# Layer 0's denominators: block sums on VectorE, and one block of row sums on TensorE in place of four

## The chip, the cores and the metric

One core of a Trainium2 chip runs the whole kernel. The time is the device time of one execution in microseconds. Three timed executions of the kernel before gave 911.12, 911.29 and 912.04 us; their median is 911.29 us. Below, PE is TensorE, DVE is VectorE, ACT is ScalarE, POOL is GpSimd and SP is SyncE, as the profile writes them.

## The reference, cut to what matters

The model has two layers over 512 tokens: layer 0 is an mLSTM mixer, layer 1 a gated linear attention. The change lies in layer 0, in the part behind the projections, which the reference writes for each of four heads in chunks:

```
s   = einsum('bhld,bhsd->bhls', q, k) * w_intra            # scores times decay weights
num = einsum('bhls,bhsv->bhlv', s, v) + ...                # numerator
den = sum(s, axis=-1) + ...                                # denominator: one number per row l
h   = num / maximum(abs(den), exp(-m_row))
```

After it come a normalisation over the 512 channels of the head, a gate with silu(z), and the output projection.

## The kernel before

The kernel takes all 512 tokens as one causal block. Tiles are held transposed: a score tile has the source position s on the 128 partitions and the target position t along the row. For a head h the causal scores are four blocks sb = 0 to 3 of source positions, kept one behind the other in one tile `A[h]` of 128 x 1280: block sb covers the targets from 128 sb to 511, so the blocks are 512, 384, 256 and 128 wide and begin at 0, 512, 896 and 1152 (`OFF`, `WID`).

All float32 products on TensorE are made from two parts, a rounded one (`hi`) and the remainder (`lo`). `split` (line 137) makes them: ACT copies the source into `hi`, then DVE subtracts `hi` from the source into `lo`. Weights that arrive by DMA are split in the same way (`whi`, `wlo`), three jobs ahead of their use.

The steps of a head, in the order in which the program writes them:

- `decay(h)` (line 661): PE forms log weights in four PSUM tiles, ACT turns them into weights `W[h]` by exp, and makes a row `EM[h]`.
- `weigh(h)` (line 678): one DVE multiplication of 128 x 1280, `A[h] = A[h] * W[h]`, with both inputs in SBUF.
- `split_scores(h)` (line 655): ACT copies `A[h]` into `shi`, DVE subtracts into `slo`.
- `split_v(h)` (line 681): ACT makes four `vhi`, DVE four `vlo`, of 128 x 512 each.
- `m_num(h)` (line 701): PE sums the rows of the scores with a matrix of ones: for each of the four blocks one matrix product with `shi` and one with `slo`, all into one PSUM tile `den`. ACT takes the absolute value `ad`, DVE the maximum with `EM[h]`. Then `attend` makes the four numerators `num`, of 12 products each; ACT squares each numerator, and POOL adds the four squares.
- `m_scale`, `m_skip` (lines 725, 735): DVE multiplies each numerator from PSUM with the gate; POOL makes four products of 128 x 512 from SBUF.
- `m_rstd(h)`, `m_y`, `y_split` (lines 742 to 768): PE sums the squares over the channels (`ssq`), DVE and ACT make the scale `rs`, DVE applies it in eight operations, and ACT and DVE split the result into `yhi` and `ylo`, the operand of the output projection `op`.

The four heads are interleaved with PE work that needs nothing of them: blocks `z` of the gate's projection (24 products of 512 columns each) behind heads 0, 1 and 2, and the first output products behind heads 2 and 3. Each engine does its own instructions in exactly the order of the program (`manual_schedule` for PE, ACT, DVE and POOL). The list of jobs sets that order: the DVE queue runs, after the numerators of head h, through a weight's `wlo`, then `weigh(h+1)` and `split_scores(h+1)`, then `rs` of head h. SBUF tiles of 128 x 512 come from one pool of 59 (`t2`), PSUM tiles from one of 8.

Of the kernel before, what the change touches and what calls it, by code (L numbers as in the profile page):

```python
# [10 lines left out]
F32R = mybir.dt.float32r  # L11
# [5 lines left out]
P = 128  # L17
T = 512
# [8 lines left out]
OFF = [0, 512, 896, 1152]  # L27
WID = [512, 384, 256, 128]
# [68 lines left out]
def tile_mlstm_gla(ctx, tc, xT, pvec, cst, wg, wgv, w_min, w_qk, w_v, w_mout,  # L97
                   w_gqk, w_gr, w_gu, w_gv, w_gz, w_gout, pw, lvl_masks, out):
    nc = tc.nc
# [9 lines left out]
    def t2(name, dt=F32):  # L109
        return tp.tile([P, T], dt, tag="t2", bufs=NT2, name=name)  # L110
# [4 lines left out]
    def t5(name, dt=F32):  # L115
        return tp.tile([P, SW], dt, tag="t5", bufs=7, name=name)

    def psum(name):
        return pp.tile([P, T], F32, tag="ps", bufs=8, name=name)

    def mm(out, lhsT, rhs, start, stop, more=False):

        nc.tensor.matmul(out, lhsT=lhsT, rhs=rhs, start=start, stop=stop, skip_group_check=more)  # L123
# [6 lines left out]
    def use(name):  # L130
        if table[0] != name:
            nc.scalar.preload_act_table_set(name)
            table[0] = name
# [3 lines left out]
    def split(hi, lo, src):  # L137
        nc.scalar.copy(hi, src)  # L138
        nc.vector.tensor_sub(lo, src, hi.bitcast(F32))  # L139
# [141 lines left out]
    ones_r = csr[:, P:2 * P]  # L281
# [131 lines left out]
    A = [None] * NH  # L413
# [239 lines left out]
    S, VS, EM = {}, {}, {}  # L653
# [2 lines left out]
        S[h] = t5("shi", F32R), t5("slo", F32R)  # L656
        split(*S[h], A[h])

    W = {}

    def decay(h):

        use(LNEXP)
        W[h] = t5("w")
        for sb in range(4):
# [4 lines left out]
            mm(ps[:, 0:P], ident_r, mneg_r, False, True)  # L670
            nc.scalar.activation(W[h][:, OFF[sb]:OFF[sb] + n], ps[:, 0:n], AF.Exp,
                                 bias=ac[:, sb * R16 + j:sb * R16 + j + 1])
# [4 lines left out]

    def weigh(h):
        nc.vector.tensor_mul(A[h], A[h], W[h])

    def split_v(h):
        VS[h] = t2s("vhi", 4, F32R), t2s("vlo", 4, F32R)
        for i in range(4):
            hi, lo = VS[h][0][i], VS[h][1][i]
            vm = vmean[:, 4 * h + i:4 * h + i + 1]
            nc.scalar.activation(hi, V[h][i], AF.Identity, bias=vm)
            nc.vector.scalar_tensor_tensor(lo, V[h][i], vm, hi.bitcast(F32), op0=ALU.add, op1=ALU.subtract)

    def attend(ps, h, vt):
        vs = slice(vt * P, (vt + 1) * P)  # L690
        (shi, slo), (vhi, vlo) = S[h], VS[h]
        for sb in range(4):
            o = ps[:, sb * P:T]
            sl = slice(OFF[sb], OFF[sb] + WID[sb])
            mm(o, vhi[sb][:, vs], shi[:, sl], sb == 0, False)
            mm(o, vhi[sb][:, vs], slo[:, sl], False, False)
            mm(o, vlo[sb][:, vs], shi[:, sl], False, sb == 3)
# [2 lines left out]

    def m_num(h):
        den = psum("den")
        shi, slo = S[h]
        for sb in range(4):
            sl = slice(OFF[sb], OFF[sb] + WID[sb])
            mm(den[:, sb * P:T], ones_r, shi[:, sl], sb == 0, False)
            mm(den[:, sb * P:T], ones_r, slo[:, sl], False, sb == 3)
        ad = t2("ad")
        nc.scalar.activation(ad, den, AF.Abs)
        nc.vector.tensor_max(ad, ad, EM[h])  # L710
        if steps:
            steps.pop(0)()
        NUM[h] = [psum("num") for _ in range(4)]
        sqs = []
        for vt in range(4):
            attend(NUM[h][vt], h, vt)
            sqs.append(t2("sq"))
            nc.scalar.square(sqs[vt], NUM[h][vt])
            if vt:
                nc.gpsimd.tensor_add(sqs[0], sqs[0], sqs[vt])  # L720
        ACC[h] = sqs[0]
        E2[h] = t2("e2")
        nc.scalar.activation(E2[h], ad, AF.Square, scale=EPS ** 0.5)
# [54 lines left out]
    job(gates3)  # L778
    z_job()
    job(lambda: (decay(0), weigh(0), split_scores(0), split_v(0)))  # L780
    job(lambda: (load_uc(0), load_uc(1)), n=0)
    z_job()
    job(lambda: load_v(1), n=0)
    job(lambda: (decay(1), steps.extend([lambda: None, lambda: (weigh(1), split_scores(1))])))

    def head_steps(h):
        m_rstd(h)
        if h + 2 < NH:
            load_v(h + 2)
            decay(h + 2)  # L790
        m_y(h, (0, 1))
        if h + 1 == NH:
            m_y(h, (2, 3))
            y_split(h, range(4))
        else:
            steps.extend([lambda: (split_v(h + 1), m_y(h, (2, 3)), silu_z(), load_uc(4 * h + 4), load_uc(4 * h + 5)),
                          lambda: None,
                          lambda: y_split(h, range(4))])
            if h + 2 < NH:
                steps.append(lambda: (weigh(h + 2), split_scores(h + 2)))  # L800
# [83 lines left out]
    for h in range(NH):  # L884
        job(lambda h=h: (m_num(h), m_scale(h), m_skip(h)), n=0)
        if h < NH - 1:
            z_job()
            job(lambda h=h: head_steps(h), n=0)
            for i in range((2, 3, 0)[h]):
                z_job(n=i < 2)  # L890
            if h == 2:
                for n in range(2):
                    out_full(n)
# [169 lines left out]
    def weights(what, c):  # L1063
        return {"P1": w_gout[0, 0, c], "P2": w_gout[0, 1, c], "P4": w_gout[1, 1, c], "P5": wsum["U", c],
                "P6": wsum["W", c], "P3": wsum["Z", c], "P7": wsum["R", c]}[what]

# [15 lines left out]
    def wsum_start(n, c):  # L1082
        nc.gpsimd.dma_start(wsum[n, c], {"U": w_gout[1, 0, c], "W": w_gout[0, 0, c], "Z": w_gout[0, 1, c],
                                       "R": w_gout[0, 0, c]}[n])

    def wsum_add(n, c):
        nc.gpsimd.dma_start(wsum[n, c], {"U": w_gout[1, 1, c], "W": wsum["U", c], "Z": wsum["W", c],
                                         "R": w_gout[1, 0, c]}[n], accum_op=ALU.add,
                            max_dma_last_dim=4096)
# [204 lines left out]
    bank, sums, parts = {}, {}, {}  # L1294
# [220 lines left out]
```

## Time and profile before

The profiled execution took 911.72 us, of which the profile's span is 910.0 us. TensorE's granted clock was at its upper level (2.4 GHz) nearly throughout.

| engine | busy us | share of the span | instructions |
|---|---|---|---|
| PE | 896.8 | 99% | 4624 |
| DVE | 628.8 | 69% | 917 |
| ACT | 539.2 | 59% | 917 |
| POOL | 182.7 | 20% | 163 |

The part that the change touches runs from about 307 to 428 us of the span, from head 0's weights to the first output products with head 3. A line of the timeline has the start in us, the duration in us, the engine, the line of the kernel, the operation, the tile written and the tiles read, and their shapes; a bracket at the end says how long the engine sat idle before and what ended that. Matrix products overlap in the pipeline, so what one costs is read from the start of one to the start of the next.

### The profile page before, as it was taken

The page shows a single profiled execution, that of the slowest core. Times are in us where ns is not written, and L with a number is a line of the kernel's source. Part 1 is how long each engine was busy: PE and PEld are TensorE (multiplying, and loading weights), DVE is VectorE, ACT ScalarE, POOL GpSimd, SP SyncE. Part 2 cuts the span into 40 slices and gives each one's busy share as a digit, 9 for nine tenths or more (in the row PEclk, how much of TensorE's full clock was granted, in tenths as well). Part 3 has the DMA queues.
Part 4 walks back from the last instruction along what each step waited for, and adds up shares of the span by engine and source line. Part 5 has one row for each costly group of instructions (what it writes and reads, how often), then busy time and mean ns, then how long its engine had stood idle before and what let it go on. Part 6 is the DMA issues. An engine that isn't in the chain of part 4 may idle for free. (4 is left out here: it accounts for less than half of the span.)

```text
span 910.0 us, 12523 instructions
## 1 busy us (share of the span) xinstructions
PE 896.8 (99%) x4624; PEld 756.1 (83%) x4624; DVE 628.8 (69%) x917; ACT 539.2 (59%) x917; POOL 182.7 (20%) x163
## 2 busy tenths in 40 slices
PE   9999999999999999999999999999999999999995
PEld 7887878878877888899999997777888888888884
DVE  6899798787695668788668748552446547478854
ACT  6866795766765657864666626455435354365642
POOL 0013564073140045135002310420000000000121
PEclk9999999999999999999999999999999999999998
DMA  8344364453432433322775694994344826383776
GB/s 320 117 163 142 125 200 136 156 189 108 149 116 94 138 116 116 115 85 88 236 226 187 210 346 150 246 240 119 116 139 127 257 101 208 115 281 108 262 277 140
DMA packets 54339, 153.88 MB, mean 169 GB/s; under 512 B 6176, under 2 KB 10656, under 8 KB 53984
## 3 DMA queue, kind: packets, MB, share of 16 engines
q1 hardware_dynamic: 48288, 126.58, 42.2%
q0 software_dynamic: 5696, 26.22, 10.9%
q8 instruction: 38, 0.62, 0.3%
q14 instruction: 29, 0.24, 0.1%
q10 hardware_dynamic: 288, 0.22, 0.1%
HBM read 133.07 MB, written 37.75 MB: 188 GB/s over the span
## 5 line engine op out<-in xcount | busy, mean ns | idle before, releaser
L139 DVE TENSOR_TENSOR wlo<-raw,whi 128x1024 fp32r<-128x1024 f32 (+1 forms) x146 | 186.3, 1283 | 96.6 <-ACT whi L138 95.8
L138 ACT CAST whi<-raw 128x1024 fp32r<-128x1024 f32 (+1 forms) x146 | 150.4, 1039 | 80.5 <-PE gv L123 24.3
L395 POOL TENSOR_TENSOR vp<-V,wv 128x512 f32<-128x512 f32 x56 | 86.2, 1560 | 173.4 <-ACT V L490 72.0
L123 PE MATMUL op<-yhi,whi 128*128 128x256 f32 x256 | 73.5, 287 | 0.0
L123 PE MATMUL op<-yhi,wlo 128*128 128x256 f32 x256 | 72.5, 283 | 0.4 <-DVE wlo L139 0.4
L123 PE MATMUL op<-ylo,whi 128*128 128x256 f32 x256 | 72.9, 285 | 0.0
L398 DVE SCALAR_TENSOR_TENSOR vp<-V,wv 128x512 f32<-128x512 f32 x72 | 68.0, 987 | 0.0
L163 POOL DMA_DIRECT2D whi<-wpP x8 | 4.3, 536 | 244.6 <-DMA raw<-in_w_gout 216.7
L123 PE MATMUL gz<-g2h,whi 128*128 128x512 f32 x128 | 51.6, 403 | 0.3 <-PEq L1180 0.3
L123 PE MATMUL qk<-chi,whi 128*128 128x512 f32 x128 | 50.1, 392 | 0.0
L123 PEld LDWEIGHTS op<-ylo,whi 128*128 128x128 f32 x256 | 49.1, 192 | 1.1 <-DVE ylo L139 0.6
L123 PE MATMUL gz<-g2h,wlo 128*128 128x512 f32 x128 | 49.9, 390 | 0.0
L123 PE MATMUL gz<-g2l,whi 128*128 128x512 f32 x128 | 49.9, 390 | 0.0
L123 PE MATMUL qk<-chi,wlo 128*128 128x512 f32 x128 | 49.8, 389 | 0.0
L123 PE MATMUL qk<-clo,whi 128*128 128x512 f32 x128 | 49.8, 389 | 0.0
L123 PE MATMUL gv<-whi,g2h 128*128 128x512 f32 x128 | 49.8, 389 | 0.0
L123 PE MATMUL gv<-wlo,g2h 128*128 128x512 f32 x128 | 49.8, 389 | 0.0
L123 PE MATMUL gv<-whi,g2l 128*128 128x512 f32 x128 | 49.8, 389 | 0.0
L123 PEld LDWEIGHTS op<-yhi,wlo 128*128 128x128 f32 x256 | 49.1, 192 | 0.6 <-DVE wlo L139 0.6
L123 PEld LDWEIGHTS op<-yhi,whi 128*128 128x128 f32 x256 | 49.1, 192 | 0.5 <-issue 0.5
L123 PE MATMUL z<-hhi,whi 128*128 128x512 f32 x112 | 44.1, 394 | 0.0
L123 PE MATMUL z<-hlo,whi 128*128 128x512 f32 x112 | 43.7, 390 | 0.0
(287 smaller groups left out, 2505.5 us busy)
## 6 DMA issues: line engine op xcount, KB each, us to landing
raw<-in_w_min SPq DMA_DIRECT2D x30, 512.0 KB, 3.8
raw<-in_w_mout SPq DMA_DIRECT2D x29, 512.0 KB, 4.2
wv<-in_wgv SPq DMA_DIRECT2D x32, 256.0 KB, 3.7
raw<-in_w_qk SPq DMA_DIRECT2D x16, 512.0 KB, 4.0
raw<-in_w_gqk SPq DMA_DIRECT2D x16, 512.0 KB, 4.3
raw<-in_w_gz SPq DMA_DIRECT2D x16, 512.0 KB, 4.7
raw<-in_w_gv SPq DMA_DIRECT2D x16, 512.0 KB, 4.1
raw<-in_w_v SPq DMA_DIRECT2D x8, 512.0 KB, 3.5
```

Source lines behind the costliest of these rows:

```text
L123: nc.tensor.matmul(out, lhsT=lhsT, rhs=rhs, start=start, stop=stop, skip_group_check=more)
L138: nc.scalar.copy(hi, src)
L139: nc.vector.tensor_sub(lo, src, hi.bitcast(F32))
L163: nc.gpsimd.dma_start(to, of)
L395: nc.gpsimd.tensor_mul(j, V[h][i], w)
L398: nc.vector.scalar_tensor_tensor(j, V[h][i], 1.0, w, op0=ALU.mult, op1=ALU.mult, accum_out=o)
```

## The change

`weigh(h)` gets six operations more. DVE adds the four blocks of the weighted scores where their targets overlap: the targets from 128 on, of block 0 and block 1 (384 columns), then block 2 (256 columns), then block 3 (128 columns). The sum `d` is split into `dsh` (ACT) and `dsl` (DVE), 384 columns each. These stand ahead of `split_scores(h)` in the order of ACT and of DVE. In `m_num(h)`, PE sums the rows of `dsh` and `dsl` for the targets from 128 on, and those of `shi` and `slo` for the first 128 targets, which block 0 alone reaches: four products in place of eight. Three more tiles of the `t2` pool are in use per head.

```
     def weigh(h):
         nc.vector.tensor_mul(A[h], A[h], W[h])
+        d, hi, lo = t2("ds"), t2("dsh", F32R), t2("dsl", F32R)
+        nc.vector.tensor_add(d[:, P:], A[h][:, P:T], A[h][:, OFF[1]:OFF[2]])
+        nc.vector.tensor_add(d[:, 2 * P:], d[:, 2 * P:], A[h][:, OFF[2]:OFF[3]])
+        nc.vector.tensor_add(d[:, 3 * P:], d[:, 3 * P:], A[h][:, OFF[3]:])
+        split(hi[:, P:], lo[:, P:], d[:, P:])
+        DS[h] = hi, lo
...
     def m_num(h):
         den = psum("den")
-        shi, slo = S[h]
-        for sb in range(4):
-            sl = slice(OFF[sb], OFF[sb] + WID[sb])
-            mm(den[:, sb * P:T], ones_r, shi[:, sl], sb == 0, False)
-            mm(den[:, sb * P:T], ones_r, slo[:, sl], False, sb == 3)
+        for sl, parts in ((slice(P, T), DS[h]), (slice(0, P), S[h])):
+            for i in range(2):
+                mm(den[:, sl], ones_r, parts[i][:, sl], i == 0, i == 1)
```

## Rows read from the trace of the kernel before

**Rows 1.** The page: span, and busy time of each engine.
```profile
span 910.0 us, 12523 instructions
...
PE 896.8 (99%) x4624; PEld 756.1 (83%) x4624; DVE 628.8 (69%) x917; ACT 539.2 (59%) x917; POOL 182.7 (20%) x163
```
**Rows 2.** Timeline of PE, head 1: the denominator, and `vlo`'s last product.
```profile
342.66 0.39 PE L123 MATMUL den<-shi,csr 128*128 128x512 f32 x1
...
343.12 0.33 PE L123 MATMUL den<-shi,csr 128*128 128x384 f32 x1
...
343.46 0.28 PE L123 MATMUL den<-shi,csr 128*128 128x256 f32 x1
...
343.70 0.22 PE L123 MATMUL den<-shi,csr 128*128 128x128 f32 x1
...
345.68 0.27 PE L123 MATMUL num<-shi,vlo 128*128 128x128 f32 x1
```
**Rows 3.** Groups by line and shape: DVE and ACT operations by their width.
```profile
L139 DVE TENSOR_TENSOR ylo<-hc,yhi 128x512 fp32r<-128x512 f32 x16 | 10.0, 687 | 0.0
...
L310 DVE TENSOR_TENSOR sq<-sq 128x256 f32<-128x256 f32 x14 | 5.9, 422 | 0.8 <-ACT sq L307 0.7
...
L547 ACT ACTIVATE A<-sc 128x384 f32<-128x384 f32 x4 | 1.9, 484 | 1.5 <-PE sc L123 1.5
```
**Rows 4.** Timeline of head 0: DVE, then PE's first use of the last `vlo`.
```profile
312.34 1.49 DVE L139 TENSOR_TENSOR slo<-A,shi 128x1280 fp32r<-128x1280 f32 x1 [1.33 <-ACT shi L138]
313.75 2.74 DVE L687 SCALAR_TENSOR_TENSOR vlo<-Vr,vmean,vhi 128x512 fp32r<-128x512 f32 x4
...
318.18 0.27 PE L123 MATMUL num<-shi,vlo 128*128 128x128 f32 x1
```
**Rows 5.** Timeline of DVE, head 1.
```profile
328.53 2.58 DVE L679 TENSOR_TENSOR A<-A,w 128x1280 f32<-128x1280 f32 x1
332.49 2.37 DVE L139 TENSOR_TENSOR slo<-A,shi 128x1280 fp32r<-128x1280 f32 x1 [1.38 <-ACT shi L138]
...
343.20 0.74 DVE L687 SCALAR_TENSOR_TENSOR vlo<-Vr,vmean,vhi 128x512 fp32r<-128x512 f32 x1
```
**Rows 6.** Timeline of POOL, head 1: the last three products of `m_skip(0)`.
```profile
327.48 2.28 POOL L740 TENSOR_TENSOR z<-ucr,z 128x512 f32<-128x512 f32 x1
...
329.73 2.53 POOL L740 TENSOR_TENSOR z<-ucr,z 128x512 f32<-128x512 f32 x1
...
332.22 1.28 POOL L740 TENSOR_TENSOR z<-ucr,z 128x512 f32<-128x512 f32 x1
```
**Rows 7.** Timeline of DVE and POOL around head 3: short DVE operations beside POOL.
```profile
407.78 2.50 DVE L139 TENSOR_TENSOR ylo<-hc,yhi 128x512 fp32r<-128x512 f32 x4
...
408.88 2.55 POOL L720 TENSOR_TENSOR sq<-sq 128x512 f32<-128x512 f32 x1 [14.84 <-ACT sq L718]
...
418.20 1.79 DVE L758 TENSOR_TENSOR hc<-hc,rs 128x512 f32<-128x512 f32 x1
```
**Rows 8.** Timeline of head 1: squares on ACT, their sum on POOL, `ssq` on PE.
```profile
350.87 2.07 ACT L718 ACTIVATE sq<-num 128x512 f32<-128x512 f32 x4
...
354.79 2.17 POOL L720 TENSOR_TENSOR sq<-sq 128x512 f32<-128x512 f32 x1
...
357.05 1.08 PE L123 MATMUL ssq<-sq,cs 128*128 128x512 f32 x2
```
**Rows 9.** Timeline of head 2: `vlo` on DVE, and PE's first use of the last.
```profile
368.34 2.73 DVE L687 SCALAR_TENSOR_TENSOR vlo<-Vr,vmean,vhi 128x512 fp32r<-128x512 f32 x4
...
378.68 0.27 PE L123 MATMUL num<-shi,vlo 128*128 128x128 f32 x1
```
**Rows 10.** Timeline behind head 3: POOL's last sum, `ssq`, PE's wait in the output.
```profile
412.88 1.29 POOL L720 TENSOR_TENSOR sq<-sq 128x512 f32<-128x512 f32 x1
...
414.24 1.11 PE L123 MATMUL ssq<-sq,cs 128*128 128x512 f32 x2
...
428.30 0.38 PE L123 MATMUL op<-yhi,wlo 128*128 128x256 f32 x1 [0.39 <-DVE wlo L139]
```

More of the change, by code (lines that the diff above doesn't have):

```diff
@@ L657, in split_scores @@
         split(*S[h], A[h])
-    W = {}
+    W, DS = {}, {}
     def decay(h):
```

## The prediction, made before the changed kernel ran

> **What bounds the kernel now.** I read the page first: TensorE is busy for 896.8 us of a span of 910.0 us [rows 1]. The reader is to see there that no other engine is near its limit, and that time taken from TensorE's queue comes off the end, as long as TensorE doesn't begin to wait. So the question is not what the added DVE and ACT work costs, but whether TensorE waits for it somewhere. For that I went from the groups by line to the timelines of the four heads, and noted for each thing that TensorE takes from the other engines how long before its use it is ready: its cover. In head 0 the last `vlo` is ready at 313.75 + 2.74 = 316.49 and first used at 318.18 [rows 4], a cover of 1.69 us. In head 1 it is ready at 343.94 and used at 345.68 [rows 2, 5]: 1.74 us. In head 2: 371.07 and 378.68 [rows 9], 7.6 us. The sum of squares that `ssq` takes is far tighter: POOL ends it at 356.96 and TensorE begins `ssq` at 357.05 [rows 8], 0.09 us later; behind head 3 the two are 414.17 and 414.24 [rows 10], 0.07 us. TensorE shows no wait there, but has no cover either.
>
> **What the change takes away.** In each head the two products of 512 columns (342.66 to 343.12, 0.46 us) and the two of 256 (343.46 to 343.70, 0.24 us) go; those of 384 and of 128 stay, with other operands [rows 2]. That is 0.70 us per head, 2.80 us for four. Weight loads lie beside the products and are not counted.
>
> **What it adds.** Three DVE additions of 384, 256 and 128 columns, an ACT copy and a DVE subtraction of 384. A DVE operation takes 0.687 us for 512 columns and 0.422 for 256 [rows 3], so by the same slope about 0.555 for 384 and 0.29 for 128; the ACT operation takes 0.48 us [rows 3]. These are 1.8 us of DVE and 0.5 us of ACT per head, and both engines have that much idle time. But they stand ahead of `split_scores`, and `shi` now waits on ACT until the additions are done and the copy `dsh` is through. Behind it in the same queues stand `slo`, `rs` of the head before, the weights of the head after, `vhi`, `vlo`, and then the denominator's `ad`, `yhi` and the squares.
>
> Head 0, with POOL silent: three additions, each begun some 0.09 us before the one ahead ends, take 1.0 us, and the copy 0.4 us more until `shi` can begin. `slo` and `vlo` come 1.4 us later. The cover of 1.69 us has shrunk by the 0.70 us that TensorE is earlier, to 0.99; TensorE waits 0.41 us. **Head 0 gains 0.29 us.**
>
> Head 1, where POOL works through its four products at the same time. The multiplication takes 2.58 us here, and `slo` 2.37 us [rows 5] where it takes 1.49 us alone [rows 4]. The rows show why: POOL's product that begins at 327.48 lasts 2.28 us, then the multiplication finishes while the next product (329.73) lasts 2.53 us, and the undisturbed last one takes 1.28 us [rows 5, 6]. The two take turns, one whole instruction each; a multiplication with both inputs in SBUF waits for a POOL product, then POOL waits for it. With the change the first addition is queued when the multiplication ends at 331.11, but POOL's product has been waiting since 329.73 and takes its turn, to 332.26. The first addition ends at about 332.66. POOL's last product, due at 332.22, now runs from there to 333.9. The second addition ends at 334.2, the third at 334.4. ACT's copy ends at 334.9 and `shi` begins at about 334.8, where it began at 331.2; it ends at 336.1. `slo` then has no POOL beside it and takes 1.49 us, to 337.6, where it ended at 334.86. **The delay is 2.75 us.**
>
> That delay stays in the chain: `rs`, the weights of head 2 and `vhi` wait behind it in turn, and ACT has no idle time up to the four squares, which run back to back at 350.87 [rows 8]. TensorE pays at two places, for the same delay and not twice. First at `vlo`: cover 1.74 less 0.70 leaves 1.04, so it waits 1.7 us in the first numerator. Then at `ssq`: POOL's sum is 2.75 us late, and TensorE begins there 2.75 - 0.09 = 2.66 us later than it did, counted from head 0's end. The 0.70 us saved in head 1 lies ahead of that wait and is lost in it. **Head 1 loses 2.66 us.**
>
> Head 2: the delay of its own additions, beside POOL again, comes on top of the first, some 5.5 to 6.7 us together. The cover of 7.6 us, less 0.70 and plus the 2.66 by which TensorE is later, still holds, and POOL there has sums only as fast as TensorE makes numerators, so that `ssq`, a whole block of `z` later, does not wait. **Head 2 gains 0.70 us.** Its numerators wait for nothing, so at their end ACT and DVE are level with TensorE again.
>
> Head 3 is as head 1: POOL's products lie beside `weigh(3)` in the same pattern. Delay 2.75 us, and `ssq` begins 2.75 - 0.07 = 2.68 us later. Here TensorE even waits now, for `wlo` at 428.30, behind head 3's `ylo` [rows 10]; that whole chain from `ssq` on moves by the same time, so nothing is won back. **Head 3 loses 2.68 us.** Past 428 us I see no cover that would take it up again, since TensorE is without pause nearly to the end.
>
> **The sum:** - 0.29 + 2.66 - 0.70 + 2.68 = +4.35 us. On the profiled execution (910.0 us of span and 1.72 around it, 911.72 us) that is 916.1 us; the median of the runs shown is 0.43 us lower, so I forecast 915.6 us.
>
> **Bounds of the unknown.** The trace holds no chain of short additions beside POOL. From below: POOL doesn't get between them at all, and the delay is that of head 0, 1.4 us. Then the sum is - 0.29 + 1.31 - 0.70 + 1.33 = +1.65 us. If POOL takes the turn after the multiplication but not between the additions, the delay in heads 1 and 3 is about 1.65 us, and the sum 2.15 us. From above: in head 3 POOL's burst itself comes late, because the squares of head 2 stand behind the delayed `yhi`; one more turn of POOL, up to 0.95 us. A `wlo` of DVE may get ahead of POOL's last sum behind head 3, 1.2 us. With eight PSUM tiles, late ACT copies of `z` can hold TensorE; I put 0.3 us, half of one such copy, as an estimate. The upper end is about +6.8 us. That a DVE addition of 0.6 us does lose its turn each time is what the row at 418.20 shows, where an operation of 0.69 us took 1.79 beside POOL [rows 7]; so I take the turns. One row speaks against them: at 408.88 POOL waited 1.3 us while DVE went on through its remaining `ylo`, and only then had its turn [rows 7].
>
> The Trainium skill, page "SBUF — State Buffer", section "Who interferes with whom", says that a DVE instruction with two SBUF inputs and a GpSimd instruction that reads SBUF exclude one another, the one that issues first going first and the other blocking fully. By that rule every turn falls as in my sum, and it speaks against this change, whose three additions all have two SBUF inputs. The row at 408.88 doesn't agree with it; by that row alone the sum would be the 2.15 us above.
>
> **Rivals.** *The cover holds.* TensorE is the busiest engine, the others have idle time, and the change brings the full 2.80 us: 908.5 us. Against it stands the 0.09 us between POOL's sum and `ssq`; it decides where the delay stays under that. Chance 0.07. *Short additions keep POOL out*, in part or wholly: +1.65 to +2.15 us, 912.9 to 913.4 us; for it speaks the row at 408.88. Chance 0.20. *Losses and gains cancel:* one of heads 1 and 3 has more cover than I read, and its 2.7 us turn into a gain of up to 0.7 or into nothing: 911 to 912 us. Chance 0.10. *More is late than I counted*, the upper bounds together or the 59 SBUF tiles running short, with three more in use per head: 917 to 918.6 us. Chance 0.15. The forecast itself, 914.5 to 917 us: 0.48.
>
> **Chances.** About 0.2% (1.8 us) is what a measurement of this kernel can tell from no change. Faster by more: the first rival, 0.07. Within: the cancelling case and the low end of the second rival, 0.13. Slower: the rest, 0.80. The range reaches from 911.6, which takes in most of the cancelling case, to 918.6.
>
> **What would show it.** In the trace of the changed kernel: four products per `den`, 0.70 us shorter; the additions of heads 1, 2 and 3 two to three times as long as those of head 0, with POOL's products between them; `slo` of head 1 ending some 2.7 us later against head 0's numerators; TensorE waiting for `vlo` in head 1 and for POOL's `sq` at two `ssq`. The prediction is wrong if TensorE shows no wait for POOL at `ssq`, or if the stretch from head 0's denominator to the `wlo` of 428.30 gets no longer.

## The result, and the profile after

The changed kernel took 917.94 us (median of six runs, 916.29 to 919.79) against 911.30 us of the kernel before: a ratio of 1.0069, 95% interval 1.0059 to 1.0079, so 6.3 us slower (5.4 to 7.2). Forecast were 915.6 us, 4.35 us slower, in a range from 911.6 to 918.6.

The page after, first two lines; they answer to [rows 1]:

```profile
span 916.0 us, 12523 instructions
...
PE 899.1 (98%) x4608; PEld 754.8 (82%) x4608; DVE 640.1 (70%) x933; ACT 540.2 (59%) x921; POOL 182.6 (20%) x163
```

TensorE has sixteen products less and 2.3 us more of busy time. Part of a wait inside a product is booked as busy, and for 3.4 us in head 3 its granted clock was at the lower level (shown further down, under head 3). Its waits tell more. The view of waits of TensorE, after (engine, line, what it waited for, us in total, times, longest):

```profile
PE num L123 <- DVE vlo L693: 2.4, 2, 1.8
...
PE ssq L123 <- POOL sq L724: 1.4, 1, 1.4
```

Neither line was there before. They are the two kinds of wait that the prediction names, but not at all its places: the two for `vlo` are in head 1 (0.56 us) and in head 3 (1.81 us), and the one for POOL's sum is behind head 1. Behind head 3 no product waits for that sum, although a second such wait was forecast; what happened there stands under head 3. The tile `ds` in the view by tile (duration in ns, least/median/greatest; first and last start):

```profile
L681 DVE TENSOR_TENSOR ds<-A x4: 558/1520/1533, 311.7 to 394.7; 128x384 f32<-128x384 f32 x4
L682 DVE TENSOR_TENSOR ds<-ds,A x4: 425/1402/1405, 312.3 to 396.2; 128x256 f32<-128x256 f32 x4
L683 DVE TENSOR_TENSOR ds<-ds,A x4: 291/778/1271, 312.8 to 397.7; 128x128 f32<-128x128 f32 x4
```

The least is head 0, without POOL; in the others the additions take up to 4.4 times as long. The timeline of DVE in head 1 shows it in order, and answers to [rows 5]:

```profile
329.41 2.58 DVE L679 TENSOR_TENSOR A<-A,w 128x1280 f32<-128x1280 f32 x1
332.02 1.52 DVE L681 TENSOR_TENSOR ds<-A 128x384 f32<-128x384 f32 x1
333.57 1.40 DVE L682 TENSOR_TENSOR ds<-ds,A 128x256 f32<-128x256 f32 x1
335.01 0.29 DVE L683 TENSOR_TENSOR ds<-ds,A 128x128 f32<-128x128 f32 x1
...
337.11 1.49 DVE L139 TENSOR_TENSOR slo<-A,shi 128x1280 fp32r<-128x1280 f32 x1 [0.61 <-ACT shi L138]
```

POOL beside it, in the same stretch, answers to [rows 6]:

```profile
330.60 2.53 POOL L744 TENSOR_TENSOR z<-ucr,z 128x512 f32<-128x512 f32 x1
...
333.08 1.61 POOL L744 TENSOR_TENSOR z<-ucr,z 128x512 f32<-128x512 f32 x1
```

Read the two together. The multiplication ends at 331.99; POOL's product, waiting since 330.60, goes first and ends at 333.13; then the first addition finishes at 333.54, 0.41 us later and 1.52 us after it began; then POOL's last product, to 334.69; then the second addition, to 334.97. The third has no POOL beside it and takes 0.29 us. From the end of the multiplication to the end of `slo` it is 6.61 us; before, it was 3.75 [rows 5]. That is the delay of head 1: 2.86 us.

The timeline of TensorE, after: what answers to [rows 2], then `ssq` behind head 1, which answers to [rows 8].

```profile
343.53 0.34 PE L123 MATMUL den<-dsh,csr 128*128 128x384 f32 x1
343.70 0.34 PE L123 MATMUL den<-dsl,csr 128*128 128x384 f32 x1
343.87 0.22 PE L123 MATMUL den<-shi,csr 128*128 128x128 f32 x1
343.93 0.27 PE L123 MATMUL den<-slo,csr 128*128 128x128 f32 x1
344.39 0.50 PE L123 MATMUL num<-shi,vhi 128*128 128x512 f32 x1 [0.18 <-ACT vhi L692]
...
345.69 0.50 PE L123 MATMUL num<-shi,vlo 128*128 128x512 f32 x1 [0.56 <-DVE vlo L693]
...
360.67 1.12 PE L123 MATMUL ssq<-sq,cs 128*128 128x512 f32 x2 [1.41 <-POOL sq L724]
```

The denominator's own products are as short as forecast. Their gain is gone within one numerator, and the wait for POOL's sum follows.

Where TensorE stands at each point, both traces, with 0.66 us taken off the starts after (by that much it was later already at head 0's weights, ahead of anything that the change touches; `dm` is the tile of log weights that `decay` makes):

| TensorE begins | before | after, shifted | later by |
|---|---|---|---|
| den, head 0 | 315.15 | 315.15 | 0.0 |
| num, head 0 | 316.37 | 315.84 | -0.5 |
| z behind head 0 | 324.05 | 324.26 | +0.2 |
| num, head 1 | 343.87 | 343.73 | -0.1 |
| z behind head 1 | 351.55 | 352.94 | +1.4 |
| dm behind ssq of head 1 | 357.57 | 360.57 | +3.0 |
| den, head 2 | 375.66 | 378.85 | +3.2 |
| num, head 2 | 376.88 | 379.37 | +2.5 |
| num, head 3 | 403.63 | 405.44 | +1.8 |
| op behind head 3 | 411.31 | 417.33 | +6.0 |
| op behind ssq of head 3 | 414.79 | 420.95 | +6.2 |
| first product of layer 1's q and k | 496.51 | 502.33 | +5.8 |

By the end of the span it is 5.3 us: the kernel before waits 0.7 us in layer 1 for DVE's `qkraw`, and the changed kernel 0.2. With the 0.66 us from ahead of the change that makes the 6.0 us between the two spans.

### The profile page after: what moved, and what is told of

Its sections match the earlier page's. It is cut to its first block, busy times and chain, and to the rows that moved or that the text cites. A ratio compares the mean times of both kernels' runs of the same rounds, so it can differ in the third digit from the quotient of the medians.

```text
span 916.0 us, 12523 instructions
## 1 busy us (share of the span) xinstructions
PE 899.1 (98%) x4608; PEld 754.8 (82%) x4608; DVE 640.1 (70%) x933; ACT 540.2 (59%) x921; POOL 182.6 (20%) x163
```

## Experiments

The theory: the added work stands ahead of `shi`, takes turns there with POOL's products, and delays a chain that reaches TensorE without cover at `ssq` behind heads 1 and 3. Rivals: TensorE alone bounds the stretch, so that its saving counts in full and the added work costs some 9 us; or the place alone costs, whatever POOL does. Each ratio is to the kernel before, timed beside the run.

**TensorE's part alone**, from the kernel after (cut; blocks 1 to 3 are left out of these denominators):

```
 def weigh(h):
     nc.vector.tensor_mul(A[h], A[h], W[h])
-    d, hi, lo = ...                        # additions and split
...
-        for sl, parts in ((slice(P, T), DS[h]), (slice(0, P), S[h])):
+        for sl, parts in ((slice(P, T), S[h]), (slice(0, P), S[h])):
```

> TensorE's part alone: four denominator products per head as in the change, but for the targets from 128 on they read block 0 of shi and slo; the block additions and their split are left out, so blocks 1 to 3 are missing from these denominators. My theory (ssq has no cover behind heads 1 and 3): heads 0 and 2 give 0.70 us each, in heads 1 and 3 all but 0.1 us is lost in a wait for POOL's sum of squares, together 1.6 us less than before, about 909.7 us, and TensorE shows a wait for POOL's sq at ssq. Rival (TensorE alone bounds this stretch, what it is spared is won in full): 2.8 us less, about 908.5 us, no such wait.

Measured: 910.69 us, ratio 0.9989 (0.9980 to 0.9998), 1.0 us faster (0.2 to 1.8). The 2.8 us of the rival are outside. TensorE's timeline, `ssq` behind head 1:

```profile
356.66 1.13 PE L123 MATMUL ssq<-sq,cs 128*128 128x512 f32 x2 [0.50 <-POOL sq L718]
```

In this trace TensorE is 1.39 us ahead at head 1's first `num`, and 0.74 at this `ssq`; 2.08 ahead at head 3's `num`, and 1.41 behind its `ssq`. So even with no added work heads 1 and 3 give next to nothing: half of what the change set out to save was never to be had.

**The sums alone**: additions and split as in the change, the eight products of before (cut).

```
-        for sl, parts in ((slice(P, T), DS[h]), (slice(0, P), S[h])):
-            for i in range(2):
-                mm(den[:, sl], ones_r, parts[i][:, sl], i == 0, i == 1)
+        for sb in range(4):
+            ...
```

> The work on VectorE and ScalarE alone: additions and split as in the change, but the denominators from all eight products per head as before (the sums are made and not used). My theory: the delay of shi, slo and what stands behind them is what costs, and TensorE's saving in heads 1 and 3 was lost in its waits anyway; so only what heads 0 and 2 saved is missing, 0.7 to 1.4 us: 7.0 to 7.7 us slower than before, about 918.3 to 919.0 us. Rival (the saving counts in full in the change and the extra work costs 2.8 us more than it brings): 6.6 + 2.8 = 9.4 us slower, about 920.7 us.

Measured: 919.79 us, ratio 1.0092 (1.0078 to 1.0106), 8.4 us slower (7.1 to 9.7). The interval touches both, so the time does not decide. The trace does: behind `ssq` of head 3 TensorE is 7.29 us late here and 6.16 with the change, so the four shorter denominators were worth at most 1.1 us there, not 2.8. Most of that is not theirs. POOL's last sum of head 3 and a `wlo` of DVE, here, and then the same sum with the change:

```profile
419.82 2.30 POOL L726 TENSOR_TENSOR sq<-sq 128x512 f32<-128x512 f32 x1
```
```profile
419.78 1.22 DVE L139 TENSOR_TENSOR wlo<-raw,whi 128x1024 fp32r<-128x1024 f32 x1
```
```profile
419.70 1.30 POOL L724 TENSOR_TENSOR sq<-sq 128x512 f32<-128x512 f32 x1
```

The `wlo` began 0.04 us ahead of the sum and cost it a turn of 1.0 us; with the change no `wlo` stood there. Without that turn the two kernels would differ by some 0.15 us at this `ssq` (an estimate). The theory had put 0.7 to 1.4 us on what heads 0 and 2 save; the 1.1 us of the trace agree in size, but come mostly from the turn.

**The change in head 2 alone** (`if h == 2:` around the additions and split and around the four products, else as before).

> The change in head 2 alone; heads 0, 1 and 3 as before. My theory: head 2 has a cover of 7.6 us between its last vlo and TensorE's use of it, three blocks of z, which holds the delay of some 3.8 us that the trace after shows there; 0.5 to 0.7 us faster than before, 910.6 to 910.8 us. Rival (additions ahead of the split cost whatever the head): a quarter of the change's loss, 1.6 us slower, about 912.9 us.

Measured: 910.90 us, ratio 0.9993 (0.9984 to 1.0002): no slower, and the rival's +1.6 us is outside. The time doesn't show a gain clear of zero; the trace has TensorE 0.44 us ahead from head 2's numerators on. Additions and split are delayed here as in the change, and the cover holds. The missing 0.25 us is a wait ahead of a block of `z`, for a PSUM tile that ACT empties late (PEld is TensorE's weight load):

```profile
365.52 0.19 PEld L123 LDWEIGHTS z<-hhi,whi 128*128 128x128 f32 x1 [0.40 <-ACT z L566]
```

**The sums later**, in heads 1 to 3, with head 0 as before (cut):

```
     def m_rstd(h):
         ...
         nc.vector.scalar_tensor_tensor(rs, ps, 1.0 / T, E2[h], ...)
+        if h + 1 < NH:
+            block_sums(h + 1)                             # the three additions
         nc.scalar.activation(rs, rs, AF.Ln, bias=tiny)
         nc.scalar.activation(rs, rs, AF.Exp, scale=-0.5)
+        if h + 1 < NH:
+            nc.scalar.copy(hi, d)                         # on 384 columns
     def head_steps(h):
         ...
         m_y(h, (0, 1))
+        if h + 1 < NH:
+            nc.vector.tensor_sub(lo, d, hi)
```

> Heads 1 to 3 with block sums, head 0 as before; the three additions stand behind the operation rs on VectorE, in the 1.5 us in which it waits for ScalarE, ScalarE's copy behind the exp of rs, the subtraction behind the first m_y. shi and slo are as early as before. My theory: the copy still delays ScalarE's chain by 0.4 us, so ssq of heads 1 and 3 begins 0.3 us later than before, head 2 gives 0.7 us: no change, 911.0 to 911.7 us. Rival (only the place ahead of shi cost something, TensorE's saving then counts in full): 3 x 0.7 = 2.1 us faster, about 909.2 us.

Measured: 911.88 us, ratio 1.0007 (0.9998 to 1.0016). The same work in heads 1 to 3, moved behind `rs`, costs next to nothing, and the whole is 6 us faster than the change. This run alone doesn't tell the place from the turns: behind `rs` most of the additions have no POOL product beside them either (in two of the three heads they take 0.54, 0.42 and 0.29 us). It gains nothing; the rival's 2.1 us are outside. `ssq` behind head 1 is 0.37 us later than before, about as expected. Behind head 3 it is 1.16 us later, where 0.3 was expected. The timelines of DVE and of POOL there:

```profile
413.59 1.21 DVE L139 TENSOR_TENSOR wlo<-raw,whi 128x1024 fp32r<-128x1024 f32 x1
```
```profile
413.63 2.29 POOL L732 TENSOR_TENSOR sq<-sq 128x512 f32<-128x512 f32 x1
```

A `wlo` began 0.04 us ahead of POOL's last sum, and that sum took 2.29 us in place of 1.29 [rows 10]. `ssq` stood behind it. One turn, lost by 0.04 us, cost 1 us.

**POOL's products moved away.** To take away the turns and leave the place, the four skip products per head were moved to DVE, behind `rs`; POOL keeps the sums of squares. The same edit was made to the kernel before and to the kernel after (cut).

```
     def m_skip(h):
         ...
-            nc.gpsimd.tensor_mul(zs[n], st["uc", n], zs[n])
     def m_rstd(h):
         ...
         nc.vector.scalar_tensor_tensor(rs, ps, 1.0 / T, E2[h], ...)
+        for n in range(4 * h, 4 * h + 4):
+            nc.vector.tensor_mul(zs[n], st["uc", n], zs[n])
```

The kernel before with it:

> The kernel before, but the four skip products per head (m_skip) run on VectorE behind rs and no longer on GpSimd; GpSimd keeps the sums of squares. My theory (GpSimd's products take turns with VectorE's multiplication and split): the multiplication takes 1.49 us in every head and slo 1.49, the chain in heads 1 and 3 comes some 3 us earlier, and TensorE loses the 1.4 us of waits in the output behind head 3: 0.5 to 1.5 us faster than before, about 910.5 us. Rival (no turns; the products just add 2.4 us to VectorE in each head): slower by 1 to 4 us.

Measured: 910.28 us, ratio 0.9983 (0.9974 to 0.9992), 1.5 us faster (0.7 to 2.4), although DVE has 2.5 us more to do per head. DVE in head 1:

```profile
328.23 1.49 DVE L679 TENSOR_TENSOR A<-A,w 128x1280 f32<-128x1280 f32 x1
331.10 1.49 DVE L139 TENSOR_TENSOR slo<-A,shi 128x1280 fp32r<-128x1280 f32 x1 [1.38 <-ACT shi L138]
332.51 0.68 DVE L751 SCALAR_TENSOR_TENSOR rs<-ssq,e 128x512 f32<-128x512 f32 x1
333.11 2.49 DVE L743 TENSOR_TENSOR z<-ucr,z 128x512 f32<-128x512 f32 x4
```

The multiplication and `slo` take 1.49 us each, which is what `slo` takes in head 0 [rows 4]; in head 1 of the kernel before they took 2.58 and 2.37 [rows 5]. The gain lies behind the heads, as expected: after `ssq` of head 3 TensorE is only 0.2 us ahead of the kernel before, at the first product of layer 1's q and k 1.6 us.

The kernel after with it:

> The change, with the skip products on VectorE as in e5_skip_dve_before. My theory: without GpSimd's products the additions take 0.56, 0.42 and 0.29 us in every head, the delay is 1.8 us, and heads 1 and 3 now have some 3 us of cover before ssq: heads 1 and 2 give 0.7 us each, head 0 loses 0.2, head 3 gives 0 to 0.7: against e5 the change is 1.2 to 1.9 us faster, about 909 us, where against the kernel before it was 6.6 us slower. Rival (the place ahead of shi costs as much without GpSimd): 4 to 7 us slower than e5.

Measured: 908.33 us, ratio 0.9961 (0.9948 to 0.9975), 3.6 us faster than the kernel before (2.3 to 4.7), and by the medians 2.0 us faster than the kernel just shown; in the traces, counted from head 0's weights to layer 1, it is 1.5 us. The additions, in the view by tile:

```profile
L681 DVE TENSOR_TENSOR ds<-A x4: 557/558/559, 311.1 to 388.3; 128x384 f32<-128x384 f32 x4
L682 DVE TENSOR_TENSOR ds<-ds,A x4: 424/426/426, 311.7 to 388.9; 128x256 f32<-128x256 f32 x4
L683 DVE TENSOR_TENSOR ds<-ds,A x4: 291/292/293, 312.2 to 389.4; 128x128 f32<-128x128 f32 x4
```

They stand at the same place as in the change, ahead of `shi`, and the same edit that costs 6.3 us beside POOL's products gains 1.5 to 2 us without them. So the place alone does not cost. Both parts of the theory are needed: the turns made the delay long, and they had eaten the cover that now holds it. No product of TensorE waits for `vlo` or for POOL's sum in heads 1 to 3 here; of the old waits 0.3 us are left, in the weight load of `ssq` behind head 3. The run also speaks against a shortage of SBUF tiles, since it needs as many of them as the change.

The last, with head 0 as before:

> As e6_skip_dve_after, but head 0 keeps its eight products and has no block sums. My theory: head 0 loses nothing, 0.2 us faster than e6, heads 1 to 3 give 0.7 us each where they have cover: 1.4 to 2.1 us faster than e5, about 908.7 us, faster than both kernels. Rival (what helped in e6 was head 0): no faster than e5.

Measured: 908.50 us, ratio 0.9965 (0.9952 to 0.9979). It beats the kernel before and the kernel before with the products moved (910.28 us), as the one above does, but these last two can't be told apart by their times. The trace has it 0.2 us ahead at `ssq` of head 3. So that head 0 loses 0.2 us with the change is read from traces alone.

## Why the prediction was right

**Which views decided.** The forecast of a loss rested on covers, not on shares of busy time: 0.09 and 0.07 us between POOL's sum and `ssq`. The run of TensorE's part alone shows that these covers were read rightly.

**The saving** was 0.70 us per denominator, as forecast: the run of TensorE's part alone gains 0.68 to 0.70 us at each of the four. With the change `den` to `num` takes 0.52 us in heads 2 and 3, where it took 1.21 before; in heads 0 and 1 a wait for what comes from the chain already lies in it.

**Head 0**: forecast a gain of 0.29, measured a loss of 0.21 us. The delay was mis-sized: 1.8 us in place of 1.4. The rows after show where:

```profile
311.70 0.56 DVE L681 TENSOR_TENSOR ds<-A 128x384 f32<-128x384 f32 x1
312.30 0.42 DVE L682 TENSOR_TENSOR ds<-ds,A 128x256 f32<-128x256 f32 x1
312.76 0.29 DVE L683 TENSOR_TENSOR ds<-ds,A 128x128 f32<-128x128 f32 x1
```

Each addition reads what the one ahead wrote, and begins 0.04 us after its end. I had taken the 0.09 us of overlap with which operations begin that don't read each other's result, such as the four `vlo`. That is 0.13 us at each of three steps.

**Head 1**: forecast 2.66 us, measured 2.79 (+0.21 to +3.0). The turns fell exactly as worked out; the delay was 2.86 us in place of 2.75.

**Head 2**: forecast a gain of 0.70, measured 0.5. The last addition lost a turn as well (1.26 us, where head 0's took 0.29), the cover held, and 0.2 us went into the late PSUM tile that stood among the upper bounds.

**Head 3**: forecast 2.68 us, measured 3.66 (+2.5 to +6.16). This term fell shortest, by one turn of POOL. The bound for it was written down (0.95 us, POOL's burst comes late because the squares of head 2 stand behind the delayed `yhi`) but not taken into the sum. DVE, then POOL:

```profile
394.67 1.53 DVE L681 TENSOR_TENSOR ds<-A 128x384 f32<-128x384 f32 x1
396.24 1.41 DVE L682 TENSOR_TENSOR ds<-ds,A 128x256 f32<-128x256 f32 x1
397.68 1.27 DVE L683 TENSOR_TENSOR ds<-ds,A 128x128 f32<-128x128 f32 x1
```
```profile
391.02 2.27 POOL L744 TENSOR_TENSOR z<-ucr,z 128x512 f32<-128x512 f32 x1
...
393.25 2.54 POOL L744 TENSOR_TENSOR z<-ucr,z 128x512 f32<-128x512 f32 x1
...
395.75 1.62 POOL L744 TENSOR_TENSOR z<-ucr,z 128x512 f32<-128x512 f32 x1
...
397.32 1.48 POOL L744 TENSOR_TENSOR z<-ucr,z 128x512 f32<-128x512 f32 x1
```

The burst begins one product late against the multiplication, so that all three additions lose a turn. From the end of the multiplication to the end of `slo` it is 7.55 us, in head 1 6.61.

TensorE came to that `ssq` by another way than forecast. It stood idle for 1.81 us at `vlo`, its longest wait in the four heads, and then ran for 3.4 us at the lower level of its granted clock (1.2 GHz); no other trace here shows that level in the heads. TensorE, and then a stretch of the view of windows (from and to in us, length, busy us and instructions of PE, PEld, DVE, ACT and POOL, granted clock, DMA share, GB/s):

```profile
408.59 0.50 PE L123 MATMUL num<-shi,vlo 128*128 128x512 f32 x1 [1.81 <-DVE vlo L693]
...
421.05 1.13 PE L123 MATMUL ssq<-sq,cs 128*128 128x512 f32 x2
```
```profile
411.00:413.00 2.00, 2.00 (x7) 1.71 (x7) 2.00 (x5) 2.00 (x5) 0.00 (x0) 0.50 0.53 202
```

At half the clock, 3.4 us of products cost some 1.7 us (an estimate). At `ssq` they cost nothing: POOL's last sum ran from 419.70 to 421.00, so TensorE would have waited for it there, as it did for 1.09 us with the sums alone. But they may have spared the kernel another turn. ACT squared the last numerator late, at 418.19, and so the `whi` and `wlo` behind it were late as well: that `wlo` began at 420.27, after POOL's last sum had started. With the sums alone, where the clock stayed up, it began 0.04 us ahead of the sum and cost it 1.0 us. The prediction has this turn among its upper bounds. With it the changed kernel would have taken some 918.9 us (917.94 and 1.0, an estimate), above the range. No run has the change without the slow stretch, so this is not shown; as far as the rows go, that the time fell inside the range is in part luck.

**The sum**: forecast +4.35, in the traces +6.16 behind head 3 and 5.3 at the end of the span (6.0 with what lay ahead of the change), timed 6.3. So some cover came after 428 us, where the forecast saw none. Of the 1.8 us that the sum was short, 1.0 are head 3's turn, 0.5 head 0, 0.2 head 2 and 0.1 head 1. The bounds as written down add up to +6.8 us, 918.1; the range reaches 0.5 us further without a term for it.

**The rivals.** The cover did not hold, short additions did not keep POOL out, and nothing cancelled. Of the upper bounds two came true in part, POOL's late burst in head 3 and the late PSUM tile in head 2.

The Trainium skill's page "SBUF — State Buffer", section "Who interferes with whom", has a DVE instruction with two SBUF inputs and a GpSimd instruction that reads SBUF block each other. The trace agrees where it matters: 0.56 us for the first addition without POOL's products, 1.52 us beside them.

## What to carry to other kernels

Work moved off the busiest engine is won only where that engine doesn't wait next: look for the smallest cover behind each place where something goes, and expect a saving ahead of a wait to be lost in it. Work put ahead of a step in another engine's queue delays everything behind it there, so ask for its place before its price; the same additions cost 6 us ahead of `shi`, beside another engine's work, and next to nothing behind `rs`. Where two engines take turns, a short instruction can cost a whole instruction of the other, so try moving the partner away: here that gained 1.5 us by itself and turned the change from a loss into a gain. And when a sum rests on who comes first by 0.04 us, forecast a range and not a number.

## What the hardware showed that I had not expected

The turns are not always fair. POOL's first sum of squares behind head 3 waited through all the remaining `ylo` of DVE, in the kernel before [rows 7] and after:

```profile
415.67 2.56 POOL L724 TENSOR_TENSOR sq<-sq 128x512 f32<-128x512 f32 x1 [16.87 <-ACT sq L722]
```

Its own work is 1.29 us, and DVE ran the rest of one `ylo` and two more of 0.68 us in the meantime, undisturbed. Beside the additions, the multiplication and `hc`, POOL had its turn after each single instruction. What tells the two cases apart was not tried and stays open.
